# A new layout of SBUF: small tiles in a first pool of 6,144 bytes, all wide tiles at multiples of 2,048

## The chip, the cores and the metric

The kernel runs on one core of a Trainium2 chip. The metric is the device time of one execution in microseconds (us); lower is better. TensorE (PE in the profile) multiplies, VectorE (DVE), ScalarE (ACT) and GpSimd (POOL) do the elementwise work, and SyncE (SP) issues most of the transfers.

## The reference

Two layers of an encoder on x of 512 x 1,024 (float32), each:

```
x = x + 0.5 * swiglu(rmsnorm(x, n1), wg1, wu1, wd1)          # 1024 -> 2816 -> 1024
proj = rmsnorm(x, nm) @ w_in                                 # 1024 -> 6800, split among the branches
mixed = g0 * (ssd(...) @ w_a) + g1 * (s5(...) @ w_b) + g2 * (retention(...) @ w_c)
x = x + mixed @ w_out
x = x + 0.5 * swiglu(rmsnorm(x, n2), wg2, wu2, wd2)
```

The gates g are sigmoids of a part of proj with a bias. After the two layers comes a last rmsnorm. Most of the arithmetic is in the matrix products with weights: the four FFNs, w_in, the three branch outputs and w_out.

## The kernel before

**Products in three matmuls.** Every float32 operand of a product with weights is split into two float32r tiles, a high and a low part, and `mm3` (lines 126 to 130) issues three matmuls: high x high, high x low, low x high. The weights come through `wload` (lines 114 to 124): SP loads a tile `wst` of up to 128 x 1,024, ScalarE casts it to `whi` (line 121) and VectorE makes the rest `wlo` (line 122). Each of the three has three buffers of 4,096 bytes a partition.

**What streams through TensorE.** In most products the weights are the stationary operand (128 columns, 512 bytes), and the activations move: 512 positions, 2,048 bytes a partition. These moving tiles are

- `hh0..7`/`hl0..7`, the normalized input x gain in two parts (`norm_k`, line 136), read by the gate and up projections of `ffn` (22 x 2 x 8 triples in each of four FFNs) and by `proj_dt` (line 330) for the gates, the convolution channels and the S5 input;
- `ah`/`al` (line 202), read by the down projections: `ffn` works in two blocks of 10 and 12 columns of 128, each with its down projection of 8 x 10 or 8 x 12 triples;
- `bh`/`bl` (branch outputs, 8 x 4, 8 x 3 and 8 x 4 triples a layer), `mh`/`ml` (w_out, 8 x 8 a layer) and `yh`/`yl` (the S5 gated unit, 3 x 2 x 3 a layer).

In `proj_td` (line 316) it is the other way around: a slice of `hh` or `hl` is stationary, and 256 columns (1,024 bytes) of `whi` or `wlo` move. In the SSD part `rb` (line 642) moves, 512 columns, 64 matmuls in all.

**Where tiles lie.** Pools are laid out in the order in which they are opened, a pool's tiles in the order of their first use, each rounded up to 32 bytes. A tag's buffers have one place each. The first pool, `c1`, begins at byte 16,512 of each partition, 128 past a multiple of 2,048. In it come `con` (3,744 bytes), `ones` (512), `x0..7` (8 x 2,048), `nmh` (256), `vec` (432, takes 448), `vec2` (304, takes 320), `s5d` (48, takes 64): 16,512 + 3,744 + 512 + 16,384 + 256 + 448 + 320 + 64 = 38,240 = 18 x 2,048 + 1,376. There `hh0`, `hl0`, `hh1`, ... begin, 16 tiles of 2,048, all at residue 1,376 of 2,048. Then `ones_r`, `ls_r`, `us_r` (512 each), `hbg` (192), `sqsum` (2,048), `rtd` (32), `rbc` (2,048): `c1` ends at 76,864. The weight pool `wp` (9 x 4,096) begins there, at residue 1,088, so a weight slice of 512 bytes lies at 1,088, 1,600, 64 or 576. `tp` holds a tile of 512 bytes for `v0`/`v3`, three `t_a` tiles of 2,048 and two `ms` of 32, and ends at 120,448, residue 1,664. All pools that follow begin there or a multiple of 2,048 behind it; the tiles of 2,048 in them that wide matmuls read (`ah`, `al`, `bh`, `bl`, `mh`, `ml`, `yh`, `yl`) are all at residue 1,664, between bytes 132,736 and about 190,000. In the SSD pool smaller tiles come first, and `rb` lies at 189,344, residue 928.

**Order.** The program's order on each engine is made by a scheduler that models the time of each instruction; waits and buffers follow from it. `c1` and `t_a` tiles are handed out in that order, a new tile of a tag waits until the last reader of the one before it in that buffer is done. SP's queue issues its transfers one after the other, and one that waits for its buffer holds those behind it.

**The start.** `load_vecs` loads `v0` (line 252), `load_x` x and the first weights (lines 232, 118), `load_consts` the rest of `con` (line 103) and casts `ones`, `ls`, `us` to float32r (lines 105 to 109), `load_vecs2` loads `v1`, `v2` (tag `t_a`, lines 262 to 265) and `v3` (line 267). `norm_sq` squares x into `t_a` tiles and adds them up on GpSimd (line 156). `norm_fin` turns the sum into `rbc` through small matmuls (line 166) and one with `ones` (line 176); the FFN needs `rbc` before it can empty a bank (line 196).

Of the kernel before, what the change touches and what calls it, by code (L numbers as in the profile page):

```python
# [10 lines left out]
F32 = mybir.dt.float32  # L11
# [7 lines left out]
P = 128  # L19
# [12 lines left out]
LAG = 400  # L32
NB = GRP // GB
# [3 lines left out]
C_ID, C_UI, C_LS, C_LI, C_US = 0, 128, 256, 384, 512  # L37
C_COS = 640
# [7 lines left out]
C_ALL = C_QT + 1024  # L46
# [33 lines left out]
class Core:  # L80
    def __init__(self, ctx, tc, consts):
        self.tc, self.nc = tc, tc.nc
        nc = self.nc
        self.c1 = ctx.enter_context(tc.tile_pool(name="c1", bufs=1))
        self.wp = ctx.enter_context(tc.tile_pool(name="wp", bufs=3))
        self.tp = ctx.enter_context(tc.tile_pool(name="tp", bufs=2))
        self.ps = ctx.enter_context(tc.tile_pool(name="ps", bufs=4, space=PSUM))
        self.dr = ctx.enter_context(tc.tile_pool(name="dr", bufs=2, space=bass.MemoryType.DRAM))
        self.con = self.c1.tile([P, C_N], F32, name="con")
        nc.sync.dma_start(self.con[:, :P], consts[:, :P])  # L90
        self.consts = consts
        self.id = self.con[:, C_ID:C_ID + P]
        self.ones = self.c1.tile([P, P], F32, name="ones")
        nc.vector.memset(self.ones, 1.0)
        self.hh = [None] * KD
        self.hl = [None] * KD
        self.x = [self.c1.tile([P, S], F32, tag=f"x{k}", name=f"x{k}") for k in range(KD)]
        self.nmh = self.c1.tile([P, 64], F32, name="nmh")
        nc.vector.memset(self.nmh, -0.5)

    def load_consts(self):
        nc = self.nc
        nc.sync.dma_start(self.con[:, P:], self.consts[:, P:C_N])
        self.ones_r = self.c1.tile([P, P], F32R, name="ones_r")
        nc.vector.tensor_copy(self.ones_r, self.ones)
        self.ls_r = self.c1.tile([P, P], F32R, name="ls_r")
        nc.vector.tensor_copy(self.ls_r, self.con[:, C_LS:C_LS + P])
        self.us_r = self.c1.tile([P, P], F32R, name="us_r")
        nc.vector.tensor_copy(self.us_r, self.con[:, C_US:C_US + P])
# [48 lines left out]
    def norm_fin(self):  # L158
# [5 lines left out]
        for t in range(NT):  # L164
            for j, a in enumerate((sh, sl)):
                nc.tensor.matmul(pb[:, 2 * t:2 * t + 2], a[:, t * P:(t + 1) * P], self.ones_r[:, :2],
                                 start=j == 0, stop=j == 1)
        ms = self.tp.tile([P, 2 * NT], F32, tag="ms", name="ms")
        nc.vector.tensor_scalar(ms, pb[:, :2 * NT], 1.0 / D, EPS, ALU.mult, ALU.add)
        self.rtd = self.c1.tile([P, NT], F32, tag="rtd", name="rtd")  # L170
# [75 lines left out]
    def load_vecs(self, i):  # L246
        nc = self.nc
        self.vec = self.c1.tile([P, 108], F32, name="vec")
        self.vec2 = self.c1.tile([P, 76], F32, name="vec2")
        self.s5d = self.c1.tile([64, 12], F32, name="s5d")  # L250
        v0 = self.tp.tile([16, P], F32, tag="v3", name="v0", bufs=1)
        nc.scalar.dma_start(v0, i["ffn1_norm"].rearrange("l (k p) -> (l k) p", p=P))
        p0 = self.bank("pa")
        nc.tensor.transpose(p0[:, :16], v0, self.id[:16, :16])
        nc.vector.tensor_copy(self.vec[:, V_N1:V_N1 + 16], p0[:, :16])

    def load_vecs2(self, i):
# [8 lines left out]
        v3 = self.tp.tile([16, P], F32, tag="v3", name="v3", bufs=1)  # L266
# [8 lines left out]
        self.hbg = self.c1.tile([P, 48], F32, name="hbg")  # L275
# [222 lines left out]
    def ssd(self, i, L, xs, hook=lambda: None):  # L498
# [4 lines left out]
        with self.tc.tile_pool(name="ssd", bufs=1) as sp:  # L503
# [35 lines left out]
            for j, m in enumerate((con[:, C_LS:C_LS + P], con[:, C_US:C_US + P], ui, li, self.ones)):  # L539
# [668 lines left out]
```

## Time and profile before

| | |
|---|---|
| median of three runs | 2,654.75 us (2,649.7 to 2,654.86) |
| span of the profiled execution | 2,647.6 us |
| PE busy | 2,591.2 us, 98% of the span, 13,040 instructions |
| PEld (weight load, overlaps PE) | 2,156.1 us, 81% |
| DVE, ACT, POOL busy | 57%, 33%, 29% |
| DMA | 286.4 MB, mean 108 GB/s |
| mean granted TensorE clock | 0.986 of full speed |

A matmul's end is modelled and reaches into the next one, so the busy time of PE says little about the pace; the start times in the timeline do. "Clock granted" is the share of 2.4 GHz that TensorE got; 0.50 is 1.2 GHz.

### The profile page before, as it was taken

What the parts mean: (1) busy time and instruction counts of PE and PEld (TensorE: products, weight loads), DVE (VectorE), ACT (ScalarE), POOL (GpSimd) and SP (SyncE); (2) the same over time, 40 slices, a digit from 0 to 9 for tenths busy, and PEclk for the clock granted to TensorE, in tenths of its full rate; (3) what the DMA queues carried; (4) which work ended last, traced back from release to release, by engine and by line L of the source; (5) the groups of instructions that cost most, each with busy time, mean ns of one, the idle gap of its engine ahead of it and who ended that gap; (6) DMA issues with size and microseconds to landing.
All of it is one profiled execution on the core that took longest, in us unless ns stands there. A gap on an engine that the chain in (4) does not pass through costs nothing.

```text
span 2647.6 us, 33895 instructions
## 1 busy us (share of the span) xinstructions
PE 2591.2 (98%) x13040; PEld 2156.1 (81%) x13040; DVE 1517.9 (57%) x2440; ACT 873.5 (33%) x1304; POOL 755.1 (29%) x824
## 2 busy tenths in 40 slices
PE   8999999999999999999999899999899999999998
PEld 6788887877899888888888688878788998888886
DVE  7644875887556644333346458668865656433433
ACT  4222443334333332222322134433333333322222
POOL 4801531462223221011114534305512323210110
PEclk9999999989999999999999999999899999999999
DMA  4353356332423332332332534554324233323322
GB/s 137 98 131 103 130 172 167 112 118 60 130 76 84 104 103 85 99 96 88 103 96 78 141 110 134 175 147 126 110 64 120 81 85 115 104 78 113 90 86 79
DMA packets 468028, 286.40 MB, mean 108 GB/s; under 512 B 43107, under 2 KB 454555, under 8 KB 467867
## 3 DMA queue, kind: packets, MB, share of 16 engines
q1 hardware_dynamic: 450219, 281.50, 36.5%
q10 hardware_dynamic: 17648, 2.75, 0.7%
q8 instruction: 102, 1.67, 0.3%
q14 instruction: 59, 0.48, 0.1%
HBM read 251.17 MB, written 29.88 MB: 106 GB/s over the span
## 4 chain that ended last, share of the span: by engine, by line
PE 85%; DVE 9%; POOL 3%; issue 1%; DMA 1%; ACT 1%; SPq 0%; ACTq 0%; DVEq 0%; POOLq 0%
PE ps_mm L130 26%; PE ps_mm L129 26%; PE ps_mm L128 26%; DVE wlo L122 1%; DVE bm L638 1%; DVE rb L644 1%; DVE cacc L566 1%; PE ps_sm L412 1%; PE ps_pa L420 1%; PE ps_sm L376 1%; PE ps_pa L419 0%; PE ps_sm L961 0%; DVE za L1024 0%; PE ps_sm L655 0%; DVE zb L1025 0%
## 5 line engine op out<-in xcount | busy, mean ns | idle before, releaser
L121 ACT ACTIVATE whi<-wst 128x1024 fp32r<-128x1024 f32 (+4 forms) x486 | 450.9, 930 | 1200.9 <-PE ps_mm L129 967.0
L130 PE MATMUL ps_mm<-hh,wlo 128*128 128x512 f32 x1936 | 774.3, 400 | 10.0 <-DVE wlo L122 10.0
L129 PE MATMUL ps_mm<-hl,whi 128*128 128x512 f32 x1936 | 775.5, 401 | 0.0
L128 PE MATMUL ps_mm<-hh,whi 128*128 128x512 f32 x1936 | 772.9, 400 | 1.7 <-DVE gt L196 1.7
L122 DVE TENSOR_TENSOR wlo<-wst,whi 128x1024 fp32r<-128x1024 f32 (+4 forms) x486 | 575.0, 1184 | 201.7 <-ACT whi L121 194.0
L130 PEld LDWEIGHTS ps_mm<-hh,wlo 128*128 128x128 f32 x1936 | 366.8, 189 | 98.1 <-DVE wlo L122 10.8
L128 PEld LDWEIGHTS ps_mm<-hh,whi 128*128 128x128 f32 x1936 | 366.8, 189 | 88.3 <-issue 2.0
L129 PEld LDWEIGHTS ps_mm<-hl,whi 128*128 128x128 f32 x1936 | 366.4, 189 | 87.4 <-issue 1.0
L199 POOL TENSOR_TENSOR sr<-gt,rbc 128x512 f32<-128x512 f32 x88 | 150.5, 1711 | 791.0 <-ACT gt L197 790.9
L130 PE MATMUL ps_mm<-ah,wlo 128*128 128x512 f32 x704 | 278.3, 395 | 2.1 <-DVE wlo L122 2.1
L129 PE MATMUL ps_mm<-al,whi 128*128 128x512 f32 x704 | 276.4, 393 | 0.0
L128 PE MATMUL ps_mm<-ah,whi 128*128 128x512 f32 x704 | 273.8, 390 | 1.5 <-ACT whi L121 1.5
L201 DVE TENSOR_TENSOR a<-ps_mm,sr 128x512 f32<-128x512 f32 x88 | 60.6, 689 | 226.9 <-PE ps_mm L130 212.4
L130 PE MATMUL ps_mm<-whi,hl 128*128 128x256 f32 x640 | 181.2, 284 | 0.0
L129 PE MATMUL ps_mm<-wlo,hh 128*128 128x256 f32 x640 | 180.9, 284 | 0.0
L128 PE MATMUL ps_mm<-whi,hh 128*128 128x256 f32 x640 | 179.4, 283 | 0.0
L196 DVE TENSOR_TENSOR gt<-ps_mm,rbc 128x512 f32<-128x512 f32 x88 | 60.2, 688 | 169.7 <-PE ps_mm L130 169.6
L128 PEld LDWEIGHTS ps_mm<-ah,whi 128*128 128x128 f32 x704 | 132.2, 188 | 30.6 <-ACT whi L121 1.9
L130 PEld LDWEIGHTS ps_mm<-ah,wlo 128*128 128x128 f32 x704 | 132.3, 188 | 30.3 <-DVE wlo L122 3.4
L129 PEld LDWEIGHTS ps_mm<-al,whi 128*128 128x128 f32 x704 | 132.2, 188 | 29.8
L130 PEld LDWEIGHTS ps_mm<-whi,hl 128*128 128x128 f32 x640 | 120.6, 188 | 2.3 <-issue 2.3
L129 PEld LDWEIGHTS ps_mm<-wlo,hh 128*128 128x128 f32 x640 | 120.7, 189 | 0.9 <-issue 0.8
(433 smaller groups left out, 3406.7 us busy)
## 6 DMA issues: line engine op xcount, KB each, us to landing
wst<-in_w_in SPq DMA_DIRECT2D x106, 512.0 KB, 3.8
wst<-in_ffn_w_gate SPq DMA_DIRECT2D x88, 512.0 KB, 3.9
wst<-in_ffn_w_up SPq DMA_DIRECT2D x88, 512.0 KB, 3.9
wst<-in_ffn_w_down SPq DMA_DIRECT2D x64, 384.0 KB, 3.5
wst<-in_ffn_w_down SPq DMA_DIRECT2D x64, 320.0 KB, 3.2
mat<-sd SPq DMA_DIRECT2D x12, 896.0 KB, 4.6
sd<-mat SPq DMA_DIRECT2D x12, 768.0 KB, 4.1
mat<-sd SPq DMA_DIRECT2D x12, 768.0 KB, 5.5
```

What stands on the lines that cost most here:

```text
L121: nc.scalar.activation(hi[:, :nk * n], sv, AF.Copy)
L122: nc.vector.tensor_tensor(lo[:, :nk * n], sv, hi[:, :nk * n].bitcast(F32), ALU.subtract)
L128: mm(out, lh, rh, start=first, stop=False)
L129: mm(out, lh, rl, start=False, stop=False)
L130: mm(out, ll, rh, start=False, stop=last)
L196: nc.vector.tensor_tensor(gt, pg, self.rbc, ALU.mult)
L199: nc.gpsimd.tensor_tensor(sr, gt, self.rbc, ALU.mult)
L201: nc.vector.tensor_tensor(a, pu, sr, ALU.mult)
L376: nc.tensor.matmul(pr[:, h * 64:(h + 1) * 64], kd[:, h].rearrange("p d e -> p (d e)"), v[:, t, h * 64:(h + 1) * 64], start=True, stop=True)
L412: nc.tensor.matmul(psc[:, h * P:(h + 1) * P], kT[:, h // 2, tc_], qT[:, h // 2, h % 2], start=True, stop=True)
L420: nc.tensor.matmul(py[:, hs], qdT[:, h * P:(h + 1) * P], st[:, t, hs], start=False, stop=True)
L566: nc.vector.scalar_tensor_tensor(acc, pad[:, j:j + S], wc[j], acc, ALU.mult, ALU.add)
```

## The change

A pool `c0` is opened ahead of `c1` and takes all small tiles: `con`, `ones`, `nmh` (padded by 88 elements), `vec`, `vec2`, `s5d`, `hbg`, `ones_r`, `ls_r`, `us_r`, `ms`, `rtd`. `con` loses the two triangles `ls` and `us` (2 x 128 columns); they come by a DMA of their own into a `t_a` tile, `tri`, and only their float32r casts stay. The matmuls at line 540 read these casts, as float32, instead. `ones_r` is cut from 128 columns to the two that are read. `v0` and `v3` lose their own tile and use the `t_a` ring of three. With that `c1`, `wp` and `tp` hold only tiles of 2,048 or 4,096 bytes.

```diff
--- before.py
+++ after.py
@@ -30,12 +30,13 @@
 BANKS = {"mm": 4, "sm": 2, "pa": 1, "pb": 1}
 XSLOT = (0, 1, 2, 11, 12, 3, 4, 5)
 LAG = 400
+PAD = 88
 NB = GRP // GB
 CH = 8
 NC = S // CH
 
-C_ID, C_UI, C_LS, C_LI, C_US = 0, 128, 256, 384, 512
-C_COS = 640
+C_ID, C_UI, C_LI = 0, 128, 256
+C_COS = 384
 C_SIN = C_COS + 128
 C_KD = C_SIN + 128
 C_GAM = C_KD + 16
@@ -43,7 +44,9 @@
 C_N = C_E16 + 16
 C_DM = C_N
 C_QT = C_DM + 1024
-C_ALL = C_QT + 1024
+C_LS = C_QT + 1024
+C_US = C_LS + 128
+C_ALL = C_US + 128
 
 
 def const_table():
@@ -81,32 +84,35 @@
     def __init__(self, ctx, tc, consts):
         self.tc, self.nc = tc, tc.nc
         nc = self.nc
+        self.c0 = ctx.enter_context(tc.tile_pool(name="c0", bufs=1))
         self.c1 = ctx.enter_context(tc.tile_pool(name="c1", bufs=1))
         self.wp = ctx.enter_context(tc.tile_pool(name="wp", bufs=3))
         self.tp = ctx.enter_context(tc.tile_pool(name="tp", bufs=2))
         self.ps = ctx.enter_context(tc.tile_pool(name="ps", bufs=4, space=PSUM))
         self.dr = ctx.enter_context(tc.tile_pool(name="dr", bufs=2, space=bass.MemoryType.DRAM))
-        self.con = self.c1.tile([P, C_N], F32, name="con")
+        self.con = self.c0.tile([P, C_N], F32, name="con")
         nc.sync.dma_start(self.con[:, :P], consts[:, :P])
         self.consts = consts
         self.id = self.con[:, C_ID:C_ID + P]
-        self.ones = self.c1.tile([P, P], F32, name="ones")
+        self.ones = self.c0.tile([P, P], F32, name="ones")
         nc.vector.memset(self.ones, 1.0)
         self.hh = [None] * KD
         self.hl = [None] * KD
         self.x = [self.c1.tile([P, S], F32, tag=f"x{k}", name=f"x{k}") for k in range(KD)]
-        self.nmh = self.c1.tile([P, 64], F32, name="nmh")
+        self.nmh = self.c0.tile([P, 64 + PAD], F32, name="nmh")
         nc.vector.memset(self.nmh, -0.5)
 
     def load_consts(self):
         nc = self.nc
         nc.sync.dma_start(self.con[:, P:], self.consts[:, P:C_N])
-        self.ones_r = self.c1.tile([P, P], F32R, name="ones_r")
-        nc.vector.tensor_copy(self.ones_r, self.ones)
-        self.ls_r = self.c1.tile([P, P], F32R, name="ls_r")
-        nc.vector.tensor_copy(self.ls_r, self.con[:, C_LS:C_LS + P])
-        self.us_r = self.c1.tile([P, P], F32R, name="us_r")
-        nc.vector.tensor_copy(self.us_r, self.con[:, C_US:C_US + P])
+        self.ones_r = self.c0.tile([P, 2], F32R, name="ones_r")
+        nc.vector.tensor_copy(self.ones_r, self.ones[:, :2])
+        tri = self.tp.tile([P, 2 * P], F32, tag="t_a", name="tri", bufs=3)
+        nc.sync.dma_start(tri, self.consts[:, C_LS:C_LS + 2 * P])
+        self.ls_r = self.c0.tile([P, P], F32R, name="ls_r")
+        nc.vector.tensor_copy(self.ls_r, tri[:, :P])
+        self.us_r = self.c0.tile([P, P], F32R, name="us_r")
+        nc.vector.tensor_copy(self.us_r, tri[:, P:])
 
     def bank(self, tag="mm"):
         return self.ps.tile([P, 512], F32, tag=tag, name=f"ps_{tag}", bufs=BANKS[tag])
@@ -163,11 +169,11 @@
         pb = self.bank("sm")
         for t in range(NT):
             for j, a in enumerate((sh, sl)):
-                nc.tensor.matmul(pb[:, 2 * t:2 * t + 2], a[:, t * P:(t + 1) * P], self.ones_r[:, :2],
+                nc.tensor.matmul(pb[:, 2 * t:2 * t + 2], a[:, t * P:(t + 1) * P], self.ones_r,
                                  start=j == 0, stop=j == 1)
-        ms = self.tp.tile([P, 2 * NT], F32, tag="ms", name="ms")
+        ms = self.c0.tile([P, 2 * NT], F32, tag="ms", name="ms", bufs=2)
         nc.vector.tensor_scalar(ms, pb[:, :2 * NT], 1.0 / D, EPS, ALU.mult, ALU.add)
-        self.rtd = self.c1.tile([P, NT], F32, tag="rtd", name="rtd")
+        self.rtd = self.c0.tile([P, NT], F32, tag="rtd", name="rtd")
         nc.gpsimd.tensor_tensor(self.rtd, ms.rearrange("p (t j) -> p t j", j=2)[:, :, 0], self.nmh[:, :NT], ALU.pow)
         dg = self.tp.tile([P, S], F32, tag="t_a", name="dg", bufs=3)
         for t in range(NT):
@@ -245,10 +251,10 @@
 
     def load_vecs(self, i):
         nc = self.nc
-        self.vec = self.c1.tile([P, 108], F32, name="vec")
-        self.vec2 = self.c1.tile([P, 76], F32, name="vec2")
-        self.s5d = self.c1.tile([64, 12], F32, name="s5d")
-        v0 = self.tp.tile([16, P], F32, tag="v3", name="v0", bufs=1)
+        self.vec = self.c0.tile([P, 108], F32, name="vec")
+        self.vec2 = self.c0.tile([P, 76], F32, name="vec2")
+        self.s5d = self.c0.tile([64, 12], F32, name="s5d")
+        v0 = self.tp.tile([16, P], F32, tag="t_a", name="v0", bufs=3)
         nc.scalar.dma_start(v0, i["ffn1_norm"].rearrange("l (k p) -> (l k) p", p=P))
         p0 = self.bank("pa")
         nc.tensor.transpose(p0[:, :16], v0, self.id[:16, :16])
@@ -263,7 +269,7 @@
         nc.sync.dma_start(v2[:60, :], i["ssd_conv_w"].rearrange("l j (k p) -> (l j k) p", p=P))
         nc.sync.dma_start(v2[60:68, :], i["ssd_norm"].rearrange("l (k p) -> (l k) p", p=P))
         nc.sync.dma_start(v2[68:76, :], i["ret_norm"].rearrange("l (k p) -> (l k) p", p=P))
-        v3 = self.tp.tile([16, P], F32, tag="v3", name="v3", bufs=1)
+        v3 = self.tp.tile([16, P], F32, tag="t_a", name="v3", bufs=3)
         nc.sync.dma_start(v3[:12, :64], i["s5_d"].rearrange("l (b g) o -> (l b) (g o)", g=GB))
         p3 = self.bank("pa")
         nc.tensor.transpose(p3[:64, :12], v3[:12, :64], self.id[:12, :12])
@@ -272,7 +278,7 @@
             pb = self.bank("pb")
             nc.tensor.transpose(pb[:, :n], v[:n, :], self.id[:n, :n])
             nc.vector.tensor_copy(o, pb[:, :n])
-        self.hbg = self.c1.tile([P, 48], F32, name="hbg")
+        self.hbg = self.c0.tile([P, 48], F32, name="hbg")
         nc.vector.tensor_scalar(self.hbg, self.vec[:, V_BG:V_BG + 48], 0.5, None, ALU.mult)
 
     def final_k(self, d, ap, g, out):
@@ -536,7 +542,7 @@
             nc.vector.tensor_tensor(dal, da, dah.bitcast(F32), ALU.subtract)
             pd = self.bank("sm")
             daf = da.rearrange("p t d -> p (t d)")
-            for j, m in enumerate((con[:, C_LS:C_LS + P], con[:, C_US:C_US + P], ui, li, self.ones)):
+            for j, m in enumerate((self.ls_r.bitcast(F32), self.us_r.bitcast(F32), ui, li, self.ones)):
                 nc.tensor.matmul(pd[:, 64 * j:64 * j + 64], m, daf, start=True, stop=True)
             dec = sp.tile([P, 5, NT, 2, 8], F32, name="dec")
             nc.scalar.activation(dec.rearrange("p j t d h -> p (j t d h)"), pd[:, :320], AF.Exp)
```

## Rows read from the trace of the kernel before

**Rows 1.** Chain of waits: share of the span by engine, from the page.

```profile
PE 85%; DVE 9%; POOL 3%; issue 1%; DMA 1%; ACT 1%; SPq 0%; ACTq 0%; DVEq 0%; POOLq 0%
```

**Rows 2.** Timeline of PE (start us, duration us): first matmuls of three stretches.

```profile
1071.60 0.40 PE L128 MATMUL ps_mm<-ah,whi 128*128 128x512 f32 x1
...
1126.54 0.40 PE L128 MATMUL ps_mm<-hh,whi 128*128 128x512 f32 x1
...
1260.94 0.39 PE L128 MATMUL ps_mm<-ah,whi 128*128 128x512 f32 x1
```

**Rows 3.** Timeline of PE, 96 to 101 us: nine matmuls lie between.

```profile
96.67 0.63 PE L128 MATMUL ps_mm<-hh,whi 128*128 128x512 f32 x1
...
100.51 0.63 PE L128 MATMUL ps_mm<-hh,whi 128*128 128x512 f32 x1
```

**Rows 4.** Windows view of the same stretch: PE busy (count), PEclk, DMA share, GB/s.

```profile
96.10:100.90 4.80, 4.80 (x11) 0.50 0.60 176
```

**Rows 5.** Timeline of PE in the second SSD part: two rb matmuls in one row.

```profile
1924.79 0.63 PE L648 MATMUL ps_sm<-rb,ls_r 128*128 128x512 f32 x2
1925.26 0.39 PE L130 MATMUL ps_mm<-hh,wlo 128*128 128x512 f32 x1
```

**Rows 6.** Timeline of PE, gate and up: first matmul of five triples.

```profile
1000.20 0.39 PE L128 MATMUL ps_mm<-hh,whi 128*128 128x512 f32 x1
...
1000.89 0.40 PE L128 MATMUL ps_mm<-hh,whi 128*128 128x512 f32 x1
...
1001.60 0.39 PE L128 MATMUL ps_mm<-hh,whi 128*128 128x512 f32 x1
...
1002.30 0.40 PE L128 MATMUL ps_mm<-hh,whi 128*128 128x512 f32 x1
...
1003.00 0.39 PE L128 MATMUL ps_mm<-hh,whi 128*128 128x512 f32 x1
```

**Rows 7.** Groups of PE by line and form: xcount | busy us, mean ns | idle.

```profile
L128 PE MATMUL ps_mm<-hh,whi 128*128 128x512 f32 x1936 | 772.9, 400 | 1.7 <-DVE gt L196 1.7
...
L128 PE MATMUL ps_mm<-ah,whi 128*128 128x512 f32 x704 | 273.8, 390 | 1.5 <-ACT whi L121 1.5
...
L128 PE MATMUL ps_mm<-whi,hh 128*128 128x256 f32 x640 | 179.4, 283 | 0.0
```

**Rows 8.** Windows view, instructions with tile hh: us, PE busy (count), the rest.

```profile
45.00:100.00 55.00, 43.67 (x133) 26.09 (x133) 0.00 (x0) 0.00 (x0) 0.93 0.22 63
498.00:626.00 128.00, 61.35 (x204) 37.02 (x202) 0.00 (x0) 0.00 (x0) 0.92 0.37 112
1425.00:1505.00 80.00, 15.21 (x48) 8.79 (x47) 0.00 (x0) 0.00 (x0) 0.99 0.44 108
1808.00:1937.00 129.00, 61.82 (x203) 37.53 (x202) 0.00 (x0) 0.00 (x0) 0.92 0.36 111
```

**Rows 9.** Timeline of PE, a projection of 256 columns: 22 starts apart.

```profile
721.89 0.28 PE L128 MATMUL ps_mm<-whi,hh 128*128 128x256 f32 x1
...
722.24 0.28 PE L128 MATMUL ps_mm<-whi,hh 128*128 128x256 f32 x1
...
722.60 0.28 PE L128 MATMUL ps_mm<-whi,hh 128*128 128x256 f32 x1
...
724.49 0.28 PE L129 MATMUL ps_mm<-wlo,hh 128*128 128x256 f32 x1
```

**Rows 10.** Timeline of SP, DVE and PE at the start.

```profile
16.62 0.30 SPq L267 DMA_DIRECT2D v<-in_s_d  x1
16.96 0.40 SPq L118 DMA_DIRECT2D wst<-in_ffn_w_gate  x1
...
19.11 0.21 DVE L109 CAST us_r<-con 128x128 fp32r<-128x128 f32 x1
...
32.39 0.16 PE L166 MATMUL ps_sm<-ones_r,sqh 128*128 128x2 f32 x1
...
43.29 0.77 PE L128 MATMUL ps_mm<-hh,whi 128*128 128x512 f32 x1 [1.68 <-DVE gt L196]
```

## The prediction

> **What bounds the kernel now.** The chain of the work that ended last comes first: by its shares TensorE carries 85% of it, VectorE 9%, GpSimd 3% [rows 1]. So nearly all of the span is a row of matmuls that follow each other without a gap, and the question is what one matmul takes from its own start to the next one's start. The durations in the profile do not tell that, since a matmul's end is modelled and overlaps the next one; the start times do. So the second view is the timeline of TensorE, at the two ends of stretches in which the program issues a known number of wide matmuls (512 columns, 2,048 bytes of the moving tile) and nothing else.
>
> The down projection of the second FFN of layer 0 issues, in its first block, 8 x 10 x 3 = 240 of them that read `ah`/`al`: 1,071.60 to 1,126.54 us, 54.94 us, **228.9 ns** each. Then come 12 x 2 x 8 x 3 = 576 of the gate and up projections that read `hh`/`hl`: to 1,260.94, 134.40 us, **233.3 ns** each [rows 2]. Same shape, same type, same weight tiles, full granted clock, no gap in either: 4.4 ns apart. What differs is the moving tile's place. From the code's sizes (worked out in the section on the kernel) `hh` and `hl` all lie at 1,376 bytes past a multiple of 2,048, and `ah`, `al`, `bh`, `bl`, `mh`, `ml`, `yh`, `yl` all at 1,664. 1,376 is 21.5 x 64; 1,664 is 26 x 64 and 13 x 128.
>
> Three more rows narrow that down. (a) In a stretch whose granted clock is 0.50 (the 1.2 GHz level; the engine had waited just before), `hh` matmuls start 3.84 us / 9 = 426.7 ns apart [rows 3, 4]; half of it is 213.3 ns. So the columns alone would take 213.3 ns at 2.4 GHz, and 20.0 ns of the 233.3 (15.6 of the 228.9) are something that only the full clock shows: an operand that does not come fast enough. (b) It is not the part of SBUF: `rb`, which lies above the `ah` tiles but at 928 = 14.5 x 64, goes at 0.47 us / 2 = 235 ns [rows 5]. (c) It is not the weights' place: the slices of `whi` lie at 64, 576, 1,088 and 1,600 past a multiple of 2,048, and four triples in a row that walk through all four take 0.69, 0.71, 0.70 and 0.70 us [rows 6].
>
> **The change part by part.** (1) *The tiles.* Every tile of the first pool is rounded up to 32 bytes: 2,720 + 512 + 608 + 448 + 320 + 64 + 192 + 32 + 512 + 512 + 2 x 32 + 32 = 6,016 bytes, and with the 128 bytes ahead of it 6,144 = 3 x 2,048. So `x`, `hh`, `hl`, `sqsum`, `rbc` (26 tiles of 2,048), the weight pool (9 of 4,096) and the three `t_a` tiles all start at residue 0, and so do all pools behind them. The padding does what it says. No matmul, vector or scalar instruction of the loops is added or taken away.
>
> (2) *The price.* The trace holds no wide read at residue 0. The nearest row is residue 1,664, a multiple of 64 and of 128, as 0 is. So I take 228.9 ns for `hh`/`hl`, a step of 4.4 ns, and nothing for the tiles that are at 1,664 now. The `hh`/`hl` matmuls are three groups of 1,936 [rows 7]: 5,808 x 4.4 ns = 25.6 us if each were on the path. They are not where the chain is not TensorE's: in four stretches (the start of the first FFN, the two SSD parts, and the end of layer 1's S5 preparation) the chain runs over VectorE and GpSimd too, whose 12% of the chain [rows 1] lie mostly there. A shorter matmul there only leaves TensorE waiting longer for the same tile. The stretches hold 133 + 204 + 48 + 203 = 588 instructions that read `hh` [rows 8]; a triple has two of `hh` and one of `hl`, so 882. Left are 4,926 x 4.4 ns = **21.7 us**.
>
> (3) *The 256-column matmuls* of the time-major projections (three groups of 640 [rows 7]) read weight slices at 64 and 1,088, multiples of 64 but not of 128, with `hh` as stationary. They start 2.60 us / 22 = 118.2 ns apart [rows 9], against half of 213.3, 106.7: 11.5 ns over 256 columns, 0.045 a column, while `hh` has 0.039 and `ah` 0.030. Per column they stand with the slow class. I take half the step for half the columns, 1,920 x 2.2 ns: **4.2 us**. The bounds are 0 (if 64 is what counts, or the weight load sets this pace) and twice that.
>
> (4) *VectorE, ScalarE, GpSimd* read and write at other residues as well. I cost that at nothing: their operands mix residues now, and together they have 12% of the chain [rows 1]. Where TensorE does not cover them, in the SSD parts, each per cent on them would be 2.6 us, since these are 257 us together [rows 8].
>
> (5) *The start.* One DMA is added to SP's queue (`tri`, the two triangles that left `con`), and `v0`, `tri`, `v3` join the ring of three `t_a` tiles in which `v1`, `v2` and the squares already turn. The load of `v3` is issued at 16.62 us now, and right behind it on SP stands a weight load at 16.96. In the new ring `v3` follows `tri`, so it can have to wait for the cast that frees `tri`, and the cast of `us_r` is at 19.11: up to 2.7 us for SP's queue, and for the weight loads behind it. The squares may lose a slot for as long. TensorE first needs their sum at 32.39, 13 us after that cast, and has gate and up matmuls until then; so I take 0. Without that cover its wait for the first banks, which ends at 43.29, grows by 2.7 us [rows 10]; a luckier order gives about as much.
>
> Sum: -21.7 - 4.2 = -25.9 us. Against the profiled execution: 2,647.6 - 25.9 = 2,621.7 us of span; the median of the three runs, 2,654.75, lies 7.2 us above that span, and I leave those 7.2 as they are: **2,628.9, say 2,629 us**.
>
> **The rivals.** *A further gain* (0.17). Residue 0 is aligned to more than 128; a read of 2,048 bytes at 1,664 still straddles a boundary of 2,048 and several finer ones. If that costs the same step again, residue 0 gives 224.5 ns for all wide reads: 4.4 ns more on the 4,926 and on 3 x 704 [rows 7] + 3 x (176 + 128 + 36) from the loops = 3,132 others, 35.5 us, thus 2,593 us. For it: 15.6 ns of the 228.9 are unexplained. Against it: the 256-column slices at 64 lie within one 2,048-byte stretch and those at 1,088 straddle two, and two triples in a row, one of each kind, take 0.35 and 0.36 us [rows 9].
> The Trainium skill ("TensorE: Matmul & The Clock Gate", Back-to-back issue gap) puts 512 columns at N/2.4 + 2.5 = 215.8 ns, whatever the address; no row here is that low, and an estimate by that page, with all wide reads on it, would be about 2,528 us.
>
> *No change* (0.16). The 4.4 ns belong to something that goes with the two groups of tiles and is not their residue; then nothing moves, 2,655 us. Against it stand (b) and (c) above.
> The Trainium skill ("SBUF — State Buffer", Specifications) gives lines of 16 bytes as what a read pays for. 1,376 and 1,664 are both multiples of 16, 128 lines each, so by that rule the change gives nothing: 2,655 us. The trace does not agree that both cost the same: 233.3 against 228.9 ns.
>
> *Slower* (0.10). Today the moving tile and the weight slice never start at the same residue of 512 (352 or 128 against 64); afterwards both always start at 0. If two streams that start alike get in each other's way, `hh` keeps its 233.3 and the 3,132 fall to it: +13.8 us, **2,669 us**. It decides as soon as the `ah` stretch is above 228.9 ns. Against it: in [rows 6] the weight slice's distance to `hh` changes by 512 at each triple and the pace does not; a distance of 0 is what no row has. A start that goes wrong (part 5) would alone stay within 2.7 us.
>
> **How the numbers follow.** The forecast has 0.54, the further gain 0.17, no change 0.16, slower 0.10; 0.03 stands for a gain of 6 to 15 us, if the SSD parts swallow more. What this measurement can tell from no change is about 0.2%, 5.3 us. Faster by more: 0.54 + 0.17 + 0.03 = 0.74; within: 0.16; slower: 0.10. The forecast's own range is 2,621 (all 5,808 on the path and 8.4 us from part 3) to 2,636 (part 3 at nothing and 2.7 us lost at the start). The range for 8 in 10 takes in no change at the top and the second step at the bottom: 2,590 to 2,660.
>
> **What would show it.** Right: the 576 matmuls between the two down projections take some 131.8 us instead of 134.40, the 240 still 54.9, and TensorE's wait in the SSD parts grows by about 1 us each. `ah` faster than 228.9 means the further gain; `ah` slower, the collision; `hh` at 233.3, that the residue is not the cause. 256-column matmuls still at 118.2 take 4.2 us off the sum. TensorE idle around 40 us by more than now means that the ring at the start costs. The step I trust least is (2)'s choice of 1,664 as the stand-in for 0.

## The result and the profile after

The changed kernel takes **2,616.72 us** (median, 2,613.18 to 2,622.1) against 2,652.22 for the kernel before, run beside it: ratio 0.9885, 95% interval 0.986 to 0.991. A second set of runs gave 2,612.5 against 2,644.07 (0.9876, 0.9856 to 0.9896). (The ratios are worked out from the single runs; the medians alone would give 0.9866 and 0.9881.) The profiled execution's span fell from 2,647.6 to 2,611.8 us, by 35.8. The forecast was 2,629: the sign was right, the gain larger by more than a third, and the reason turned out to be another one than the forecast gives.

The chain of waits of the changed kernel, shares of the span by engine, answers to [rows 1]:

```profile
PE 82%; DVE 10%; POOL 3%; issue 2%; DMA 1%; ACT 1%; SPq 0%; ACTq 0%; DVEq 0%; POOLq 0%
```

TensorE still sets the end. The groups of PE by line, xcount | busy us, mean ns | idle us before them, answer to [rows 7] (all lines of `mm3` stand 6 lower now):

```profile
L134 PE MATMUL ps_mm<-hh,whi 128*128 128x512 f32 x1936 | 761.4, 394 | 0.5 <-DVE gt L202 0.5
...
L134 PE MATMUL ps_mm<-ah,whi 128*128 128x512 f32 x704 | 275.2, 392 | 0.9 <-ACT whi L127 0.9
...
L134 PE MATMUL ps_mm<-whi,hh 128*128 128x256 f32 x640 | 180.6, 285 | 0.0
```

The counts are the same; the `hh` group is 11.5 us less busy, and the 256-column group, against the forecast, 1.2 us more. As before, the mean of one instruction is no pace; the starts are. The timeline of PE (start us, duration us) at the ends of the same stretches as in [rows 2], and at the end of the second `ah` block:

```profile
1061.64 0.39 PE L134 MATMUL ps_mm<-ah,whi 128*128 128x512 f32 x1
...
1116.04 0.39 PE L134 MATMUL ps_mm<-hh,whi 128*128 128x512 f32 x1
...
1246.60 0.39 PE L134 MATMUL ps_mm<-ah,whi 128*128 128x512 f32 x1
...
1311.88 0.39 PE L134 MATMUL ps_mm<-hh,whi 128*128 128x512 f32 x1
```

240 `ah` matmuls in 54.40 us, 576 of `hh` in 130.56, 288 of `ah` in 65.28: **226.67 ns** each in all three. `hh` gained 6.66 ns, not 4.4, and the tiles that were to stay at 228.9 gained 2.2. The same holds for `mh` (192 matmuls, 43.52 us, 226.67 ns), `bh` and `yh`. The 256-column projection [rows 9], from its first matmul to the one behind its last, 194 in all:

```profile
714.75 0.28 PE L134 MATMUL ps_mm<-whi,hh 128*128 128x256 f32 x1
...
738.02 0.27 PE L377 MATMUL ps_sm<-con,rot 128*128 128x128 f32 x1
```

23.27 / 194 = 119.95 ns, against 22.96 / 194 = 118.35 in the same stretch before (721.18 to 744.14 us). This part got slower. At the start nothing was lost: the matmul of [rows 10] that waited for the first free banks until 43.29 us now starts at 42.40.

```profile
42.40 0.50 PE L134 MATMUL ps_mm<-hh,whi 128*128 128x512 f32 x1 [0.49 <-DVE gt L202]
```

With the forecast's own counts the paces give -6.66 x 4,926 - 2.2 x 3,132 + 1.6 x 1,920 = -32.8 - 6.9 + 3.1 = -36.6 us, beside -35.8 of the spans. That the two agree so well is partly luck, since two stretches of the kernel vary from execution to execution (last section).

### The profile page after: what moved, and what is told of

The parts are those of the page before. It is cut to its first block, busy times and chain, and to the rows that moved or that the text cites. A ratio compares the mean times of both kernels' runs of the same rounds, so it can differ in the third digit from the quotient of the medians.

```text
span 2611.8 us, 33899 instructions
## 1 busy us (share of the span) xinstructions
PE 2551.9 (98%) x13040; PEld 2158.0 (83%) x13040; DVE 1517.7 (58%) x2440; ACT 872.1 (33%) x1304; POOL 753.8 (29%) x824
## 4 chain that ended last, share of the span: by engine, by line
PE 82%; DVE 10%; POOL 3%; issue 2%; DMA 1%; ACT 1%; SPq 0%; ACTq 0%; DVEq 0%; POOLq 0%
PE ps_mm L136 25%; PE ps_mm L135 25%; PE ps_mm L134 25%; DVE wlo L128 1%; DVE rb L650 1%; DVE bm L644 1%; DVE cacc L572 1%; PE ps_sm L418 1%; PE ps_pa L426 1%; PE ps_sm L382 1%; PE ps_pa L425 1%; DMA sd<-mat 0%; DVE za L1030 0%; DVE zb L1031 0%; DMA braw<-in_s_b_im 0%
## 5 line engine op out<-in xcount | busy, mean ns | idle before, releaser
L136 PE MATMUL ps_mm<-hh,wlo 128*128 128x512 f32 x1936 | 763.4, 394 | 9.4 <-DVE wlo L128 9.4
L135 PE MATMUL ps_mm<-hl,whi 128*128 128x512 f32 x1936 | 764.5, 395 | 0.0
L134 PE MATMUL ps_mm<-hh,whi 128*128 128x512 f32 x1936 | 761.4, 394 | 0.5 <-DVE gt L202 0.5
L136 PEld LDWEIGHTS ps_mm<-hh,wlo 128*128 128x128 f32 x1936 | 366.3, 189 | 86.1 <-DVE wlo L128 10.7
L207 DVE TENSOR_TENSOR a<-ps_mm,sr 128x512 f32<-128x512 f32 x88 | 60.6, 689 | 213.3 <-PE ps_mm L136 195.2
```

The lines of the kernel that those rows point to most:

```text
L134: mm(out, lh, rh, start=first, stop=False)
L135: mm(out, lh, rl, start=False, stop=False)
L136: mm(out, ll, rh, start=False, stop=last)
L207: nc.vector.tensor_tensor(a, pu, sr, ALU.mult)
```

## The experiments

Theory A is the forecast's: the residue of the moving tile itself sets the pace. Its rivals came from two readings: that the gain lies in something else that the layout moved (C, G), and that the *distance* between the moving tile and the stationary one counts (D). B, E and F are variants of A; H to K belong to experiments 7 and 9. Distances below are the moving tile's address less the stationary tile's, and are worked out from the layout of each kernel.

**1. `hh` alone put back.**

```diff
-PAD = 88
+PAD = 0
-        self.rbc = self.c1.tile([P, S], F32, tag="rbc", name="rbc")
+        self.rbc = self.c1.tile([P, S + 88], F32, tag="rbc", name="rbc")[:, :S]
```

> The pad of 352 bytes moves from the first pool to behind `rbc`: `x`, `hh`, `hl`, `sqsum` and `rbc` lie at residue 1,696 again (a remainder of 32 after division by 64, as 1,376 had), all else stays at 0. Theory A (the address of the moving tile alone sets the pace of a wide matmul, and step (2) was right in kind but too small): matmuls that read hh/hl go back from 226.67 to 233.3 ns, 6.66 ns x 4,926 = 32.8 us, so about 2,649 us, while those that read ah, bh, mh and yh stay at 226.67. Rival B (step (2) as on record, 4.4 ns): 21.7 us, about 2,638. Rival C (the gain comes from the other tiles, the weights and the small tiles, and hh's own place is worth nothing): 2,617, hh at 226.67. For the 256-column matmuls, whose stationary tile is hh and whose moving tile is `whi`: back from 119.96 to 118.3 ns if hh's place sets them, 119.96 if that of `whi` does.

Measured: 2,644.7 us, 0.9988 of the kernel before (0.9973 to 1.0002); span 2,647.7. The timeline of its PE:

```profile
1072.17 0.39 PE L134 MATMUL ps_mm<-ah,whi 128*128 128x512 f32 x1
...
1126.57 0.40 PE L134 MATMUL ps_mm<-hh,whi 128*128 128x512 f32 x1
...
1261.51 0.39 PE L134 MATMUL ps_mm<-ah,whi 128*128 128x512 f32 x1
```

`hh`: 134.94 / 576 = 234.3 ns; `ah`: 54.40 / 240 = 226.67. All of the gain is gone, and C with it. But A and D both said so. The 256-column matmuls stay at 120.0, although `hh`, their stationary tile, has moved away.

**2. All but `hh` put back.**

```diff
-        self.rbc = self.c1.tile([P, S], F32, tag="rbc", name="rbc")
+        self.rbc = self.c1.tile([P, S + 416], F32, tag="rbc", name="rbc")[:, :S]
```

> 1,664 bytes behind `rbc`: `hh`, `hl` stay at residue 0, all tiles behind them, the weights, ah, bh, mh and yh among them, lie at 1,664, where ah and its like lay before. Theory A (the moving tile's own address): hh stays at 226.67 ns, the others go back from 226.67 to 228.9, 2.25 ns x 3,132 = 7.0 us, about 2,624 us. Rival D (what counts is the distance between the moving and the stationary tile): hh, now 1,664 away from its weights, slows to between 228.9 and 233.3, 11 to 33 us, 2,628 to 2,650, and ah, still level with its weights, keeps 226.67. Rival E (anything on a multiple of 64 or 128 is as good as 0): nothing changes, 2,617. 256-column matmuls: 118.3 if the place of `whi` sets them, 119.96 if that of hh does.

Measured: 2,634.58 us, 0.9963 (0.9944 to 0.9982); span 2,630.4. Its PE:

```profile
1059.92 0.39 PE L134 MATMUL ps_mm<-ah,whi 128*128 128x512 f32 x1
...
1114.34 0.40 PE L134 MATMUL ps_mm<-hh,whi 128*128 128x512 f32 x1
...
1248.73 0.39 PE L134 MATMUL ps_mm<-ah,whi 128*128 128x512 f32 x1
```

This is where A falls, and E with it. `hh` lies at residue 0 and takes 134.39 / 576 = **233.3** ns; `ah` lies at 1,664, where it had 228.9 before the change, and takes 54.42 / 240 = 226.75. Not the place of the moving tile, but its distance to the weights decides: 0 for `ah` here, -1,664 for `hh`. (By these paces the span would be some 4 us below the 2,647.6 of the kernel before, and it is 17 below. Most of the rest lies in the two stretches with the SSD parts, which took 461.4 and 463.1 us against 470.5 and 466.4. That is not the chance of one execution alone: the interval of the seven runs lies wholly below the 0.9986 that the paces give. The mean granted clock was 0.99 in five of the seven, and in two of the 18 runs of the kernel before. Why this layout has it, no run shows; the last section comes back to these stretches.)

**3. Weights scattered, two kernels.** In the first the weight buffers lie at 0, 32 and 64 (`whi`) and 128, 160 and 192 (`wlo`), in the second at 64, 128, 192 and 256, 320, 384, with `hh` at 32; pads of the following kind do it.

```diff
-        hi = self.wp.tile([P, 1024], F32R, tag="whi", name="whi")
+        hi = self.wp.tile([P, 1032], F32R, tag="whi", name="whi")
```

> One look, a table of paces: hh at 0; the three `whi` buffers at 0, 32 and 64, the three `wlo` buffers at 128, 160 and 192; ah at 256, 224, 384 and 192 in the four FFNs; bh and yh at 192; mh at 512 and 1,024. Theory A: each pace goes by the moving tile's residue alone, so hh 226.67 with every weight buffer; ah at 224 near 233; the others between 226.67 and 228.9 by how high a power of two divides their residue (192: 228.9 or more; 256, 384, 512, 1,024: if 128 decides all are 226.67 but then 1,664 would have been too, so at 384 228.9 and at 512 and 1,024 226.67 is the likelier). Rival D (distance): within one FFN the pace changes from weight buffer to weight buffer. Rival F (the stationary tile's address counts too): hh at 0 has 226.67 with the buffers at 0, 64, 128, 192 and more with those at 32 and 160, by up to 5 ns, as `dtw2` at 672 shows 231.65 with hh at 0. Time: 3,000 to 4,000 wide matmuls by 0 to 7 ns more, 2,617 to 2,640 us.

> One look, a table of paces: hh at 32; `whi` at 64, 128 and 192, `wlo` at 256, 320 and 384; ah at 512, 480, 0 and 576 in the four FFNs; bh at 448 and 480; mh at 448 and 512; yh at 448 and 480. Theory A (moving tile's residue alone): hh 233.3, ah at 512 and 0 226.67, at 480 233.3, at 576 (a multiple of 64) 228.9 or more. Rival D (distance): hh, 32 away from a buffer at 64, differs from one buffer to the next. Rival F (stationary address counts too): with all weights on multiples of 64 nothing of it shows here, and ah at 0 and 512 keeps 226.67. 256-column matmuls: `whi` at 64, 128 and 192 with hh stationary at 32. Time: 4,926 x 6.66 = 33 us more for hh and 0 to 10 for the others, 2,648 to 2,660 us.

Measured: 2,653.88 and 2,646.28 us. PE of the first:

```profile
1126.24 0.40 PE L135 MATMUL ps_mm<-hh,whi 128*128 128x512 f32 x1
...
1259.99 0.39 PE L135 MATMUL ps_mm<-ah,whi 128*128 128x512 f32 x1
```

`hh` at 0: 133.75 / 576 = 232.2 ns, `ah` in both kernels 231.7 to 232.9. No stretch was at 226.67, whatever the moving tile's residue: A and F had `hh` at or near it in the first kernel, and A the `ah` at 0 and 512 in the second. With three buffers at different distances in turn the pace changes from buffer to buffer (in this stretch of the first kernel 233.2, 232.0 and 231.5 ns in turn, means of 24 matmuls), so the price of one distance can't be read here. In the next kernels all weights are alike.

**4. Everything shifted by the same amount.** The one line that fills the first pool up is taken out:

```diff
-PAD = 88
+PAD = 0
```

> The pad of 352 bytes is taken out: every tile behind the first pool, `hh`, the weights, ah, bh, mh and yh alike, lies at residue 1,696 (a remainder of 32 after division by 64), so nothing a wide matmul reads is on a multiple of 64, but moving and stationary tiles have the same residue. Theory D (what counts is that the moving and the stationary tile agree, distance 0): every wide matmul at 226.67 ns, as in the changed kernel, about 2,617 us, profiled span 2,612. Theory A (each tile's own multiple of 2,048, or of 64, counts): every wide matmul at the pace of hh in `hhback`, 234.3 ns or near it, 7.6 ns x 8,058 = 61 us more, about 2,675.

> The changed kernel as it is, on the same chip as `shiftall`, for a comparison side by side: 2,617 us by every theory; its 256-column matmuls at 119.8 ns.

Measured: 2,619.05 us, 0.9896 (0.9874 to 0.9919), next to 2,612.5 and 0.9876 (0.9856 to 0.9896) for the changed kernel; the intervals overlap and the spans are 2,606.1 and 2,610.7. Its PE:

```profile
1055.13 0.39 PE L134 MATMUL ps_mm<-ah,whi 128*128 128x512 f32 x1
...
1109.53 0.39 PE L134 MATMUL ps_mm<-hh,whi 128*128 128x512 f32 x1
...
1240.09 0.39 PE L134 MATMUL ps_mm<-ah,whi 128*128 128x512 f32 x1
```

54.40 / 240 and 130.56 / 576: 226.67 ns with every tile at residue 1,696, which is no multiple of 64. The multiple of 2,048 in the change is not needed; that all tiles have the *same* residue is.

**5. A table of distances.** Weights at one residue, and `hh`, `ah`, `bh`, `mh`, `yh` each at another, by pads ahead of the first tile of a group, as in

```diff
-                h = ap.tile([P, S], F32R, tag=f"ah{m - m0}", name="ah")
+                o = off if m == m0 else 0
+                h = ap.tile([P, S + o], F32R, tag=f"ah{m - m0}", name="ah")[:, o:]
```

> One look, a table of pace by distance, taken as the moving tile's address less that of its weights, both modulo 512 (the slices of a weight tile lie 512 bytes apart). All weights at 256. hh at 0: distance 256. ah at 320, 384, 512 and 704 in the four FFNs: 64, 128, 256 and 448. mh at 288 and 272: 32 and 16. bh at 448 and 576: 192 and 320. Theory D: every distance that isn't 0 is slower than 226.67, at 64 it is 228.9 as ah had before the change, elsewhere between 228.9 and 234.5; equal distances give equal paces in hh and ah (256). Theory A: hh at 0 and ah at 512 have 226.67. Open, and no theory gives it: whether a distance is faster than 0. Time by D 5,808 hh by some 6 ns and 2,500 others by some 5: 2,655 to 2,665 us; under A about 2,630.

> One look, the second half of the table. All weights at 64. hh at 0: distance 448. ah at 80, 96, 448 and 256: distances 16, 32, 384 and 192. mh at 72 and 480: 8 and 416. bh at 160 and 352: 96 and 288. Theory D: 384 gives 233.3 as hh had in `restback`, 288 gives 233.3 as hh had before the change; small distances (8, 16, 32) between 226.67 and 234; equal distances give equal paces with those of the other table (32, 16 close by; 192 and 448 the same). Theory A: hh at 0 has 226.67, ah at 256 and 448 too or 228.9. Time by D 2,640 to 2,665 us.

Measured: 2,626.75 and 2,659.82 us. The first was 30 us below what D gave, and the reason is in its timeline:

```profile
1058.25 0.40 PE L135 MATMUL ps_mm<-ah,whi 128*128 128x512 f32 x1
...
1114.24 0.39 PE L135 MATMUL ps_mm<-hh,whi 128*128 128x512 f32 x1
...
1244.81 0.40 PE L135 MATMUL ps_mm<-ah,whi 128*128 128x512 f32 x1
...
1312.00 0.39 PE L135 MATMUL ps_mm<-hh,whi 128*128 128x512 f32 x1
```

`hh`, 256 away from its weights, takes 130.57 / 576 = 226.68 ns, while `ah`, 128 away, takes 67.19 / 288 = 233.3. So the pattern repeats every **256 bytes**, not 512. The second kernel, `ah` 32 away from its weights:

```profile
1262.05 0.39 PE L135 MATMUL ps_mm<-ah,whi 128*128 128x512 f32 x1
...
1329.24 0.39 PE L135 MATMUL ps_mm<-hh,whi 128*128 128x512 f32 x1
```

67.19 / 288 = 233.3. (Of the distances 16 and 8 nothing was learned: behind the first tile of a group the tiles are rounded up to 32 bytes, so nearly all lay at 32.)

**6. The gain without the new layout.** The kernel before, with 32 bytes behind `rbc` and 192 in the small tile `v3`, and nothing moved:

```diff
-        self.rbc = self.c1.tile([P, S], F32, tag="rbc", name="rbc")
+        self.rbc = self.c1.tile([P, S + 8], F32, tag="rbc", name="rbc")[:, :S]
-        v3 = self.tp.tile([16, P], F32, tag="v3", name="v3", bufs=1)
+        v3 = self.tp.tile([16, P + 48], F32, tag="v3", name="v3", bufs=1)[:, :P]
```

(`v0`, which shares the tag, gets the same pad.)

> The kernel before, with nothing moved: 32 bytes behind `rbc` and 192 bytes in the small tile `v3`. By the table so far the pace repeats every 256 bytes, and before the change hh lay at 96, the weights at 64 and ah, bh, mh, yh at 128 modulo 256; the two pads put all of them at 96. Theory D (distance, modulo 256): every wide matmul at 226.67 ns and the whole gain of the change without its new layout, some 2,612 to 2,619 us, ratio about 0.988; 256-column matmuls at 119.96 ns, as at distance 0 in the changed kernel. Rival A (multiples of 64 or 2,048 count): all at 233 or more, 4 ns x 3,132 more than before, about 2,660 us. Rival G (the small tiles' own pool, or the shorter constants, give part of the gain): between, 2,625 to 2,640.

Measured: 2,619.45 us against 2,649.22, ratio **0.9881** (0.9859 to 0.9904), the same as the change's.

```profile
1062.18 0.39 PE L128 MATMUL ps_mm<-ah,whi 128*128 128x512 f32 x1
...
1116.58 0.39 PE L128 MATMUL ps_mm<-hh,whi 128*128 128x512 f32 x1
...
1247.14 0.39 PE L128 MATMUL ps_mm<-ah,whi 128*128 128x512 f32 x1
```

226.67 ns in both stretches, with `hh` at 1,376, the weights at 1,120 and `ah` at 1,888, all 96 modulo 256. Rivals A and G are out: 224 bytes of padding give the whole gain of the change, as far as these intervals tell.

**7. Which of the two reads is disturbed.**

```diff
-        lo = self.wp.tile([P, 1024], F32R, tag="wlo", name="wlo")
+        lo = self.wp.tile([P, 1024 + 64], F32R, tag="wlo", name="wlo")[:, 32:1056]
```

> One look. In the changed kernel each `wlo` buffer's data lie 128 bytes on, so of the three matmuls of a step two have a stationary tile at distance 0 and the third, hh with `wlo`, at 128. While one matmul streams, the weights of the next are loaded. Theory H (the load of the next weights and the stream of the current matmul disturb each other): of the three the second is slow, hl with `whi`, under which `wlo` is loaded: some 233 ns, the other two near 226.67, mean about 229, time about 2,635 us. Theory I (the distance of a matmul's own two tiles): the third is slow instead. Theory J (any mixture sets all three off): mean 231 to 233 over all three, as in `map1`, time about 2,650 us.

Measured: 2,646.15 us, nearer to J's time than to H's. One step of three in its timeline, and the first matmul of the next:

```profile
1195.21 0.39 PE L134 MATMUL ps_mm<-hh,whi 128*128 128x512 f32 x1
1195.43 0.40 PE L135 MATMUL ps_mm<-hl,whi 128*128 128x512 f32 x1
1195.67 0.40 PE L136 MATMUL ps_mm<-hh,wlo 128*128 128x512 f32 x1
1195.90 0.39 PE L134 MATMUL ps_mm<-hh,whi 128*128 128x512 f32 x1
```

A step takes 0.69 us, 693.3 ns (three times 231.11, the mean of the `hh` stretch) against 680. From start to start over the whole kernel (medians): the first 227 ns, the second, under which the displaced `wlo` is loaded, 232, the third, which multiplies by it, 234. So H and I each name one of two that are slow, and J is wrong, since the first is untouched. One displaced tile costs 13.3 ns a step, twice the 6.66 that a matmul loses where all tiles lie off (experiment 2): as if it counted once while it is loaded and once while it is used. The load of `wlo` itself is no longer than in the changed kernel, 188 ns (lines view, mean ns behind the busy time):

```profile
L136 PEld LDWEIGHTS ps_mm<-hh,wlo 128*128 128x128 f32 x159 | 29.9, 188 | 6.2
```

It ends some 41 ns before the third matmul starts (median), so the third does not wait for a longer load. Why the third is slow, while the tile loaded under it lies at distance 0, stays open, and so does whether the 232 ns of the second are a slower stream of its own or a later start of the third.

**8. The rest of the table, and the projections.** The weights of the 256-column projections start 0, 32, 64 to 224 bytes on in their buffers, in turn:

```diff
+        o = 0
+        if n == 256:
+            self.npj += 1
+            o = 8 * (((self.npj - 1) // 2) % 8)
-        hi = self.wp.tile([P, 1024], F32R, tag="whi", name="whi")
+        hi = self.wp.tile([P, 1024 + 64], F32R, tag="whi", name="whi")[:, o:o + 1024]
```

(`wlo` alike; `ah` is displaced by pads as in 5.)

> One look, the rest of the table. The changed kernel with the weights of the 256-column projections 0, 32, 64 to 224 bytes on, in turn from projection to projection, hh at 0: pace of a 256-column matmul by distance. So far 0: 119.96, 64: 117.8, 128: 120.0, 224: 118.3. Expected: 64 the fastest or near it, a gain of some 2.2 ns against 0; 0 and 128 the slowest. ah at 224, 96, 128 and 160 in the four FFNs (512 columns): 233.3 each, and 234.3 at 160, as hh had there. Time: ah 1,950 x 6.7 ns = 13 us more than the changed kernel and 1 to 3 us less from the projections, about 2,625 us.

Measured: 2,627.04 us. `ah`, 96 away:

```profile
1246.26 0.40 PE L140 MATMUL ps_mm<-ah,whi 128*128 128x512 f32 x1
...
1313.47 0.40 PE L140 MATMUL ps_mm<-hh,whi 128*128 128x512 f32 x1
```

67.21 us for 288 matmuls, 233.4 ns each. All that the runs say about distance, modulo 256, each from a long unbroken stretch of a kernel where there is one (256 columns: `hh` is the stationary tile, weights move):

| distance | 512 columns, ns | from | 256 columns, ns | from |
|---|---|---|---|---|
| 0 | 226.67 | changed, 1, 2, 4, 6 (and `hh` 256 away in 5: 226.68) | 119.96 | changed, 4, 6 |
| 32 | 233.3 | before (`hh`), 5 (`ah`, `mh`) | 117.8 | 8 |
| 64 | 228.9 | before (`ah`), 5 (`ah`) | 117.8, single rows 113.3 | 5, 8 |
| 96 | 233.3 to 233.4 | 5 (`bh`), 8 (`ah`) | 119.9 to 120.0 | 1, 8 |
| 128 | 233.3 | 2 (`hh`), 5, 8 (`ah`) | 119.9 to 120.0 | 2, 8 |
| 160 | 234.3 | 1 (`hh`), 5 (`mh`), 8 (`ah`) | 117.3 | 8 |
| 192 | 233.3 | 5 (`hh`, `ah`) | 114.0 (32 matmuls), 117.8 (194) | 8, 9 |
| 224 | 233.2 (short rows only) | 8 (`ah`) | 118.3 | before, 8 |

For the wide matmuls 0 is the best of the eight. For the 256-column ones it is among the worst. But there the distance alone does not set the pace. In the second kernel of experiment 5 all weights lie at 64, and two rows of 256-column matmuls, one behind the other with four other matmuls between, go like this (timeline of PE):

```profile
764.75 0.28 PE L136 MATMUL ps_mm<-wlo,hh 128*128 128x256 f32 x1
...
770.64 0.28 PE L135 MATMUL ps_mm<-whi,hh 128*128 128x256 f32 x1
...
771.31 0.28 PE L137 MATMUL ps_mm<-whi,hl 128*128 128x256 f32 x1
...
774.94 0.28 PE L135 MATMUL ps_mm<-whi,hh 128*128 128x256 f32 x1
```

5.89 / 50 = 117.8 ns and 3.63 / 32 = 113.4 ns at the same distance. The lowest entry of the table, 114.0 at 192, comes from such a row of 32. It was tried in a kernel of its own.

**9. A version with both.**

```diff
+        o = 48 if n == 256 else 0
-        hi = self.wp.tile([P, 1024], F32R, tag="whi", name="whi")
+        hi = self.wp.tile([P, 1024 + 64], F32R, tag="whi", name="whi")[:, o:o + 1024]
```

(and `wlo` alike)

> The changed kernel with the weights of the 256-column projections 192 bytes on in their buffers, all else as it is: wide matmuls at distance 0, 256-column ones at distance 192, where the table had its lowest pace, 114.0 to 114.6 ns against 119.8 at distance 0. If the projections go at TensorE's pace (1,702 of their 1,920 matmuls run in unbroken rows): 5.2 to 5.8 ns x 1,920 = 10 to 11 us less than the changed kernel, some 2,602 to 2,607 us, ratio to the kernel before about 0.984. Rival K (the 134 matmuls of that row of the table were a lucky stretch, or the next weights arrive too late for the faster pace): 0 to 4 us less, 2,610 to 2,617 us.

Measured: 2,611.11 us, ratio 0.9853 (0.9828 to 0.9879); span 2,614.1. Against the changed kernel (0.9876, 0.9856 to 0.9896) that is not a difference. The projection:

```profile
714.37 0.28 PE L135 MATMUL ps_mm<-whi,hh 128*128 128x256 f32 x1
...
737.22 0.27 PE L378 MATMUL ps_sm<-con,rot 128*128 128x128 f32 x1
```

22.85 / 194 = 117.8 ns, not 114: rival K. All weights of these matmuls lie at 192 now, and yet their rows have one of two paces: of the 38 unbroken rows of 16 matmuls or more, 22 settle at 113.3 ns and 16 at 117.8, and none changes on its way. Two rows of the first layer have 117.8 where the same part of the program in the second layer has 113.3, so what decides lies ahead of the row, and no run shows what it is. Over all matmuls in unbroken rows the mean is 116.3 against 119.8. The following stretch of projections shows the gain, from 738.02 to 907.47 us in the changed kernel (169.4) and from 737.22 to 904.72 here (167.5), 1.9 us a layer, with 0.4 from the 194 above; 4.6 us in two layers, less than the executions of one kernel differ.

## Why the prediction was right, and where it was wrong

**What bounds the kernel**: right. TensorE's pace from start to start moved and the time moved with it: between the forecast's two down projections in layer 0 nothing else changed, 134.40 to 130.56 us.

**Step (1), the tiles**: right by the layout, the tiles that it lists are at residue 0; but that is not what counts (experiments 2 and 4).

**Step (2), the price**: the kind of cost was right, its cause wrong. The step that failed is (c), "it is not the weights' place". It watched four weight slices that lie 512 bytes apart [rows 6], and since the pattern repeats every 256, they all had the same distance to `hh`. The row could not have shown what it was taken to rule out. Before the change `hh` lay 288 from its weights, which is 32, and `ah` 576, which is 64: 233.3 and 228.9 in the table. So 1,664 was no stand-in for 0. At the measured paces the term -4.4 ns x 4,926 becomes -6.66 ns x 4,926, 32.8 us for 21.7, and the tiles costed at nothing give -2.2 ns x 3,132 = -6.9 us. That the sign came right is luck as far as the reason goes: with `hh` at 0 and the weights at 1,664, both multiples of 64, `hh` gains nothing (experiment 2). The new layout helped because it put both operands at one residue. What the forecast named as a sign in the stretches with waits proves nothing: TensorE's idle time in them went from 11.0 and 10.1 us to 12.9 and 10.6, about as forecast, but it is 13.3 and 12.8 in experiment 6, at the same paces (last section). (b), the pace of `rb` [rows 5], is left open: its distance is 64 and two matmuls took 235 ns each, but none of its 64 stand in a long unbroken row.

**Step (3), the 256 columns**: wrong in sign. -4.2 us were forecast; at the measured paces it is +1.6 ns x 1,920 = +3.1. "Per column they stand with the slow class" carried the price of a moving 512-column tile over to matmuls whose pattern is another one: the table's two columns do not rise and fall together.

**Step (4)**: nothing measured speaks against 0, and nothing shows it, as the SSD stretches vary too much. **Step (5)**: right in size, the first banks came 0.9 us earlier. The wait that it feared did not come about, as the order changed: `v3` is issued 2.1 us later, at 18.70 us, but now behind the weight loads, the first of which goes out at 16.42 instead of 16.96.

**The rivals.** *A further gain* (0.17) had its mark, `ah` below 228.9, come true, but by another mechanism: 226.67, not 224.5, and at 1,696 as well as at 0. Of (a)'s 20.0 ns beyond the 213.3 of the columns, 13.3 are still there at distance 0, and no run here says what they are. *Slower* had named the right variable, the distance between the two streams, with the wrong sign; it rested on "a distance of 0 is what no row has", and that was the unknown which should have moved chance to both sides. Of the two sentences on the Trainium skill: by the lines of 16 bytes ("SBUF — State Buffer", Specifications) all layouts here cost the same, since every tile lies on a multiple of 16; the rows differ by up to 7.6 ns. The 215.8 ns of the Trainium skill ("TensorE: Matmul & The Clock Gate", Back-to-back issue gap), which that section gives for a matmul by itself, were reached by no stretch of any kernel; 226.67 was the lowest.

**The sum**: 2,628.9 was 12 us too high: 11.1 from `hh`, 6.9 from the other wide tiles, less 7.3 from the projections (+3.1 for -4.2), is 10.7. The rest is less than executions of one kernel differ.

## What to carry to other kernels

When two groups of equal matmuls have different paces at the full clock and without gaps, work out the addresses of *both* operands of each, and compare their distance, not each one's alignment: in this kernel 224 bytes of padding in two places were worth 30 us of 2,650. A reading that rules a cause out must vary that cause by steps that could show it; slices 512 bytes apart could not show a pattern of 256. And a pace belongs to one shape: what helped 512 columns slowed 256 down. All this is measured for float32r, a stationary tile of 128 x 128 and tiles at multiples of 32 bytes.

## What the runs showed of the hardware

**The pace of a wide matmul hangs on the distance of its two operands modulo 256 bytes.** The weight load of the next matmul starts with the stream of the current one: in the timeline of the changed kernel PEld's row starts within 0.01 us of PE's.

```profile
1200.36 0.39 PE L134 MATMUL ps_mm<-hh,whi 128*128 128x512 f32 x1
1200.36 0.19 PEld L135 LDWEIGHTS ps_mm<-hl,whi 128*128 128x128 f32 x1
1200.58 0.39 PE L135 MATMUL ps_mm<-hl,whi 128*128 128x512 f32 x1
```

With both at the same residue of 256 a float32r matmul of 512 columns starts each 226.67 ns, at 64 each 228.9, at any other multiple of 32 each 233.2 to 234.3. The Trainium skill ("TensorE: Matmul & The Clock Gate", Step-by-step: what each phase is for) says that loading the next tile's weights takes nothing from the read bandwidth of the running matmul. Experiment 7 speaks against that: the second matmul of its step has its own two tiles at distance 0, only the tile loaded under it lies elsewhere, and the next start comes after 232 ns instead of 227. Whether it is the read of the running matmul that suffers, no run here shows.

**Stretches with waits vary between executions at equal paces.** The two stretches from the end of the first FFN to the first 256-column projection, of the kernel before, the changed kernel and experiment 6 in the windows view (us, PE busy, PEld, DVE, ACT and POOL busy, PEclk, DMA share, GB/s):

```profile
250.70:721.20 470.50, 459.47 (x2367) 379.14 (x2366) 348.68 (x546) 174.26 (x269) 171.73 (x186) 0.97 0.43 126
1560.60:2027.00 466.40, 456.33 (x2366) 376.76 (x2365) 349.45 (x546) 174.26 (x268) 172.52 (x186) 0.98 0.43 127
```

```profile
247.60:714.70 467.10, 454.20 (x2366) 379.97 (x2365) 349.44 (x546) 174.03 (x268) 172.04 (x186) 0.97 0.42 127
1540.90:1999.90 459.00, 448.40 (x2366) 375.35 (x2365) 349.84 (x546) 174.31 (x268) 171.75 (x186) 0.98 0.43 129
```

```profile
246.40:715.30 468.90, 455.65 (x2367) 380.56 (x2366) 349.42 (x546) 174.17 (x268) 171.98 (x186) 0.97 0.43 127
1541.20:2008.50 467.30, 454.52 (x2366) 380.01 (x2365) 349.63 (x546) 174.12 (x268) 172.09 (x186) 0.97 0.43 127
```

The second ones of the last two, whose paces are equal, differ by 8.3 us. TensorE waits in the SSD part there, and behind it the clock came back at different times. In the changed kernel the granted clock is 1.00 from 1,900 us on, in the other 0.95 up to 2,008; of the 8 us between the two windows below 5.4 are busy time at the lower clock and 2.6 are waits:

```profile
1900.00:2000.00 100.00, 99.18 (x468) 82.58 (x467) 63.74 (x98) 39.09 (x71) 18.40 (x21) 1.00 0.36 100
```

```profile
1900.00:2008.00 108.00, 104.54 (x469) 86.65 (x468) 66.81 (x102) 39.51 (x71) 21.91 (x24) 0.95 0.33 93
```

That is why spans of single executions here tell no differences under some 10 us apart, while the pace of an unbroken stretch of wide matmuls repeats to about 0.1 ns.
